# Transposing an 8192 x 8192 matrix: each DMA engine takes every sixteenth row of a chunk, and a permutation matrix on TensorE restores the order

## The chip, the cores and the metric

The kernel runs on one core of one Trainium2 chip. The metric is the device time in microseconds (us) of one execution; lower is better. The kernel before took 1264.38 us, the median of three runs between 1263.99 and 1264.57 us. Its profile comes from one execution of its own.

## The reference

```python
x = np.random.randn(8192, 8192).astype(np.float32)

def reference(x):
    return np.transpose(x)
```

Input and output are 268.4 MB each and both lie in HBM. There is no arithmetic to do: every number is read once, moved to its transposed place and written once.

## The kernel before

The matrix is cut into 128 chunks of 128 rows by 4096 columns (2 MB each): two column halves `s`, and 64 row blocks `c` in each. The list `chunks` (line 98) goes through all row blocks of the left half and then all of the right half. A chunk passes through four stages.

**Load** (`load`, lines 100 to 104). One DMA brings a chunk into one of three SBUF buffers `ins`, one row of x for each of the 128 partitions, 16 KB contiguous on both sides. The first three loads are issued on SP's queue, the other 125 on ScalarE's. Load t+3 is issued (lines 241 to 243) once TensorE has done the last transpose of chunk t, which frees the buffer.

**Transpose** (`transposes`, lines 111 to 124). TensorE waits for the chunk's load (line 112), then makes 32 transposes of 128 x 128: a matmul with the matrix `ident`, which GpSimd builds once at the start (lines 86 to 96). The chunk's columns are taken in 8 groups `q` of 512; within a group, transpose `b` takes every fourth column. The results go to PSUM, groups 0 to 3 to one half (`ps0`), 4 to 7 to the other (`ps1`); before each half TensorE waits until the half's last copies are done (line 116). TensorE runs this as a loop over three buffers (lines 138 to 149); the other engines' programs are written out in full.

**Copy** (lines 185 to 238). ScalarE copies the first half of PSUM, VectorE the second, into one of nine SBUF regions `regs`. A region gathers, for one group of 512 columns, what up to eight consecutive row blocks give, so that an output row gets a contiguous piece of up to 1024 numbers (4 KB). The group number sets at which row block its region closes (line 195), so that in the steady run about one region closes with each chunk. Before a region is filled anew, the copying engine waits until the region's last store has landed (line 202).

**Store** (`store`, lines 160 to 179). A closed region goes out as one DMA on ScalarE's queue. `wide_dma` (lines 25 to 36) writes the instruction directly, so that SBUF's side stays 16 KB contiguous per partition while the output's side has four rows of 4 KB. Only the first store is an ordinary one (line 174).

So loads and stores, but for the first three loads, are issued on ScalarE's queue, in the order of the program there: the copies of a chunk, the stores of the regions that these close, the next load. At the end SP waits for all stores (line 245).

The change touches the building of `ident` and `load`. What its steps meet are the DMA queues, the transposes of line 118 that read both, and the waits of lines 112, 202 and 242.

Of the kernel before, what the change touches and what calls it, by code (L numbers as in the profile page):

```python
# [40 lines left out]
def kernel(  # L41
# [14 lines left out]
    P = 128  # L56
# [8 lines left out]
    NIN = 3  # L65
    NREG = 9
    CH = N // P
    J = S * P

    with tc.tile_critical():  # L70
        nc.alloc_sbuf_tensor("pad", [P, 32], dt)
        ident = nc.alloc_sbuf_tensor("ident", [P, P], dt).ap()
        ins = [nc.alloc_sbuf_tensor(f"in{k}", [P, J], dt).ap() for k in range(NIN)]
        SIZE = B * W * P
# [10 lines left out]

        nc.gpsimd.memset(ident, 0.0).then_inc(s_id, 1)  # L86
        nc.gpsimd.wait_ge(s_id, 1)
        nc.gpsimd.affine_select(  # L88
            out=ident,
            in_=ident,  # L90
            compare_op=mybir.AluOpType.not_equal,
            fill=1.0,
            base=0,
            pattern=[[-1, P]],
            channel_multiplier=1,
        ).then_inc(s_id, 1)

        chunks = [(s, c) for s in range(M // J) for c in range(CH)]

        def load(t):  # L100
            s, c = chunks[t]
            (nc.sync if t < NIN else nc.scalar).dma_start(
                out=ins[t % NIN], in_=x[c * P:(c + 1) * P, s * J:(s + 1) * J]
            ).then_inc(s_ld[t % NIN], 16)


# [45 lines left out]
        for t in range(NIN):  # L152
            load(t)
# [6 lines left out]
        def store(q, e, count):  # L160
# [3 lines left out]
            for s, a, z in parts:  # L164
                rows = (z - a) * P
                j0 = s * J + q * B * P
                dst = out[j0:j0 + B * P, a * P:a * P + rows]
# [17 lines left out]
        for t, (s, c) in enumerate(chunks):  # L185
            for e in range(2):
# [3 lines left out]
                for q in range(e * NH, (e + 1) * NH):  # L190
# [13 lines left out]
                    k = [p[0] for p in parts].index(s)  # L204
                    base = r * SIZE + B * P * sum(z - a for _, a, z in parts[:k])
                    _, a, z = parts[k]
# [13 lines left out]
                for u in runs:  # L220
# [4 lines left out]
                    i = pss[e][:, u[0] * B * P:(u[-1] + 1) * B * P]  # L225
                    i = i.rearrange("p (l b i) -> p l b i", b=B, i=P)
# [14 lines left out]
            if t + NIN < T:  # L241
                nc.scalar.wait_ge(s_pe, (t + 1) * NR // 2)
                load(t + NIN)
# [32 lines left out]
```

## Time and profile before

| | before |
|---|---|
| median of three runs | 1264.38 us |
| the profiled execution: span from first to last instruction | 1261.2 us |
| TensorE matmul / weight load busy | 740.3 us (59%) / 719.8 us (57%) |
| VectorE / ScalarE busy | 302.7 us (24%) / 252.6 us (20%) |
| mean granted TensorE clock | 0.751 |
| DMA packets, bytes, mean rate | 39273, 536.97 MB, 426 GB/s |

The page comes from one execution; its span leaves out what lies before the first and after the last instruction. The kernel's time is some 3 us above that span. Busy time of an engine says how long it had work in hand, not that the kernel waited for it. DMA is not an engine with a program of its own: a transfer is issued by SP or ScalarE, waits in a queue, and is carried out by sixteen DMA engines together, each of them taking a share. The page shows how busy these sixteen were in 40 slices of the span, and how long a transfer took from its issue to its landing. Beside the page, the trace holds one record for each packet that a DMA engine moved, with its start, its length in time and its bytes, and one for each of the sixteen steps by which a transfer raises its semaphore. It does not say which of the sixteen a packet belongs to; since an engine's next packet starts 3 to 4 ns before the last one ends, the packets can be strung together into sixteen chains.

### The profile page before, as it was taken

The page shows a single profiled execution, that of the slowest core. Times are in us where ns is not written, and L with a number is a line of the kernel's source. Part 1 is how long each engine was busy: PE and PEld are TensorE (multiplying, and loading weights), DVE is VectorE, ACT ScalarE, POOL GpSimd, SP SyncE. Part 2 cuts the span into 40 slices and gives each one's busy share as a digit, 9 for nine tenths or more (in the row PEclk, how much of TensorE's full clock was granted, in tenths as well). Part 3 has the DMA queues.
Part 4 walks back from the last instruction along what each step waited for, and adds up shares of the span by engine and source line. Part 5 has one row for each costly group of instructions (what it writes and reads, how often), then busy time and mean ns, then how long its engine had stood idle before and what let it go on. Part 6 is the DMA issues. An engine that isn't in the chain of part 4 may idle for free. (4 is left out here: it accounts for less than half of the span.)

```text
span 1261.2 us, 9840 instructions
## 1 busy us (share of the span) xinstructions
PE 740.3 (59%) x4096; PEld 719.8 (57%) x4096; DVE 302.7 (24%) x250; ACT 252.6 (20%) x257; POOL 0.7 (0%) x6
## 2 busy tenths in 40 slices
PE   6555655665556565665555655656566655656561
PEld 6555555665556555655555655656566655656561
DVE  3322222222222222222222222222222222222220
ACT  3212121121111211122211121121111211122120
POOL 0000000000000000000000000000000000000000
PEclk9987867777776868687776777676867677777866
DMA  9999999999999999999999999999999999999998
GB/s 386 429 427 426 430 427 429 431 428 430 431 428 431 429 429 430 430 429 430 425 423 419 431 430 429 430 430 429 431 430 429 431 429 430 430 430 429 429 429 351
DMA packets 39273, 536.97 MB, mean 426 GB/s; under 512 B 4320, under 2 KB 4832, under 8 KB 6240
## 3 DMA queue, kind: packets, MB, share of 16 engines
q10 hardware_dynamic: 38832, 530.60, 98.9%
q1 hardware_dynamic: 432, 6.29, 1.2%
q14 instruction: 8, 0.07, 0.0%
q8 instruction: 1, 0.02, 0.0%
HBM read 268.44 MB, written 268.44 MB: 426 GB/s over the span
## 5 line engine op out<-in xcount | busy, mean ns | idle before, releaser
L118 PE MATMUL ps<-ident,in 128*128 128x128 f32 x4096 | 740.3, 363 | 492.9 <-PEq L116 492.9
L118 PEld LDWEIGHTS ps<-ident,in 128*128 128x128 f32 x4096 | 719.8, 220 | 513.2 <-issue 513.2
L228 DVE COPY regs<-ps 128x512 f32<-128x512 f32 (+3 forms) x250 | 302.7, 1246 | 932.4 <-PE ps L118 780.2
L228 ACT COPY regs<-ps 128x512 f32<-128x512 f32 (+3 forms) x256 | 251.3, 1015 | 980.9 <-PE ps L118 495.5
L228 ACT ACT_TABLE_LOAD x1 | 1.3, 1283 | 0.9 <-SPq L70 0.9
L88 POOL TENSOR_SCALAR_AFFINE_SELECT ident<-ident 128x128 f32<-128x128 f32 x1 | 0.3, 292 | 0.2 <-POOL ident L86 0.2
L86 POOL MEMSET ident<- 128x128 f32 x1 | 0.2, 204 | 0.5 <-SPq L70 0.5
L260 POOL MEMSET const-bfloat16-1.0<- 128x1 bf16 x1 | 0.1, 101 | 0.0
L260 POOL MEMSET const-uint8-127<- 128x1 uint8 x1 | 0.1, 101 | 0.0
L260 POOL MEMSET const-float32-0.0<- 128x1 f32 x1 | 0.1, 98 | 0.2 <-issue 0.2
L260 POOL MEMSET const-float32-1.0<- 128x1 f32 x1 | 0.1, 98 | 0.0
## 6 DMA issues: line engine op xcount, KB each, us to landing
in<-in_x_dram ACTq DMA_DIRECT2D x125, 2048.0 KB, 21.7
out_dram<-regs ACTq DMA_DIRECT2D x114, 2048.0 KB, 17.5
out_dram<-regs ACTq DMA_DIRECT2D x4, 1792.0 KB, 17.1
in<-in_x_dram SPq DMA_DIRECT2D x3, 2048.0 KB, 11.6
out_dram<-regs ACTq DMA_DIRECT2D x4, 1536.0 KB, 15.2
out_dram<-regs ACTq DMA_DIRECT2D x4, 1280.0 KB, 15.5
out_dram<-regs ACTq DMA_DIRECT2D x4, 1024.0 KB, 15.6
out_dram<-regs ACTq DMA_DIRECT2D x4, 768.0 KB, 16.5
```

Source lines behind the costliest of these rows:

```text
L86: nc.gpsimd.memset(ident, 0.0).then_inc(s_id, 1)
L88: nc.gpsimd.affine_select(out=ident, in_=ident, compare_op=mybir.AluOpType.not_equal, fill=1.0, base=0, pattern=[[-1, P]], channel_multipl ...
L118: tr = nc.tensor.transpose(pss[e][:, (g * B + b) * P:(g * B + b + 1) * P], ins[k][:, q * B * P + b:(q + 1) * B * P - B + b + 1:B], ident,)
L228: cp = nc.scalar.copy(out=o, in_=i) if e == 0 else nc.vector.tensor_copy(out=o, in_=i)
L260: nc = _bacc.Bacc("TRN2", target_bir_lowering=False, num_devices=1)
```

## The change

The source of a load is presented in another order. Before, partition p of a buffer receives row p of the chunk, and rows and partitions are both one dimension of 128. Afterwards the source has two dimensions for the rows, 16 outer ones in steps of one row and 8 inner ones in steps of sixteen rows; the destination stays 128 partitions in sequence. Partition 8k + i therefore receives row 16i + k. The diff's sense is that each of the sixteen DMA engines takes one k, that is every sixteenth row. The matrix with which TensorE transposes is no longer the identity but the permutation that puts the rows back: in row 8k + i its one stands in column 16i + k. So PSUM holds the same numbers as before, and everything behind it is the same. A helper `split` is added and not called.

```diff
+    E = 16
...
         nc.gpsimd.memset(ident, 0.0).then_inc(s_id, 1)
         nc.gpsimd.wait_ge(s_id, 1)
+        shaped = ident.rearrange("p (i k) -> p i k", k=E)
         nc.gpsimd.affine_select(
-            out=ident,
-            in_=ident,
+            out=shaped,
+            in_=shaped,
             compare_op=mybir.AluOpType.not_equal,
             fill=1.0,
             base=0,
-            pattern=[[-1, P]],
+            pattern=[[-1, P // E], [-(P // E), E]],
             channel_multiplier=1,
         ).then_inc(s_id, 1)

         chunks = [(s, c) for s in range(M // J) for c in range(CH)]
+
+        def split(a):
+            step, n = a.ap[0]
+            return bass.AP(a.tensor, a.offset, [[step * (n // E), E], [step, n // E]] + [list(d) for d in a.ap[1:]])

         def load(t):
             s, c = chunks[t]
             (nc.sync if t < NIN else nc.scalar).dma_start(
-                out=ins[t % NIN], in_=x[c * P:(c + 1) * P, s * J:(s + 1) * J]
+                out=ins[t % NIN],
+                in_=x[c * P:(c + 1) * P, s * J:(s + 1) * J].rearrange("(i k) j -> k i j", k=E),
             ).then_inc(s_ld[t % NIN], 16)
```

## The prediction

> **What bounds the kernel now.** I read the page's parts 2 and 3 first (slices and queues), then part 6 (issues), then the total of the waits, then windows cut around the stages.
>
> ```profile
> DMA  9999999999999999999999999999999999999998
> GB/s 386 429 427 426 430 427 429 431 428 430 431 428 431 429 429 430 430 429 430 425 423 419 431 430 429 430 430 429 431 430 429 431 429 430 430 430 429 429 429 351
> ...
> q10 hardware_dynamic: 38832, 530.60, 98.9%
> q1 hardware_dynamic: 432, 6.29, 1.2%
> ```
>
> The sixteen DMA engines are busy in every slice, and the two queues together take 100.1% of sixteen engines' span. The rate is flat near 430 GB/s, whatever the compute engines do. Nothing on TensorE, VectorE or ScalarE sets the end (59%, 24% and 20% busy on the page).
>
> ```profile
> in<-in_x_dram ACTq DMA_DIRECT2D x125, 2048.0 KB, 21.7
> out_dram<-regs ACTq DMA_DIRECT2D x114, 2048.0 KB, 17.5
> ...
> in<-in_x_dram SPq DMA_DIRECT2D x3, 2048.0 KB, 11.6
> ```
>
> A 2 MB load lands 21.7 us after its issue, though 2.097 MB at 430 GB/s is 4.9 us: it stands behind about 16.8 us of other transfers. The queue is over three transfers deep.
>
> ```profile
> ACT regs L228 <- PE ps L118: 495.5, 100, 9.2
> PE ps L118 <- PEq L116: 492.9, 127, 8.5
> ACT regs L228 <- DMA out_dram<-regs: 473.9, 60, 10.4
> ```
>
> In the totals of the waits, everything on the compute side waits for a transfer or for something that waited for one.
>
> ```profile
> 4.00:10.00 6.00, 1.00 1.01 434
> 300.00:400.00 100.00, 0.72 1.01 430
> 640.00:700.00 60.00, 0.72 1.01 421
> 1238.00:1248.00 10.00, 0.50 1.01 421
> ```
>
> These windows (start and end, us, granted clock, DMA share, GB/s) hold loads alone, the mix, the middle with its cut stores, and stores alone. Loads alone are no faster than the mix. So the end is the sum of the packets' times on one engine, and only a change in those can move it.
>
> The trace's single packet records give that sum. Each load puts 8 packets of 16,384 B on each engine; a packet takes 611 ns, and the next starts 3 to 4 ns before its end, so 0.607 us each. 128 loads are 1,024 packets, 622 us of an engine; the stores (2 at 611 ns, 6 at 616) are the same again. 622 + 627 = 1249 us; with first packets of up to 1.46 us, 9 ns for each semaphore write and 5.3 us by which the last engine lags at the end, this fills 1261.2 us. The median, 1264.38 us, is 3.2 us above this span; I carry those 3.2 us.
>
> **The change, part by part.**
>
> Identity (lines 86 to 96). The same single select of 128x128 on GpSimd with a two-dimensional pattern. Now 292 ns, over 1.66 us into the span; the first weight load waits for data until 8.43 us. Even if it doubled, 6.8 us of the first load cover it: 0.
>
> TensorE (lines 111 to 124). 4096 matmuls of 128x128 f32 before and after, same operands, same order, one matrix with its ones elsewhere: 0. They are 740.3 us in a span of 1261.2, behind loads.
>
> Issue of the loads. Three on SP's queue (1.32 us together) and 125 on ScalarE's (0.33 to 0.8 us each). The new source has three dimensions (16 by 8 rows by 4096), as the stores have at line 28, whose issue takes 0.55 us. Say +0.25 us each: 125 x 0.25 = 31 us on ScalarE's queue. Behind a load's issue stand the next ScalarE copies and store issues, which idle 473.9 + 495.5 us. The 16.8 us of queued transfers hide it; without that cover it would be the 31 us. The first load's issue alone is bare: +0.3 us.
>
> Packets of the loads, the one term that counts. A row's 4096 elements stay contiguous on both sides, so I expect 128 packets of 16 KB per load as now, 8 for each of 16 engines (16 divides the new outer 16 and the 128 partitions). [...]
>
> What the rows cannot say is which partitions an engine writes now. In the first load all sixteen engines start within 0.9 us and finish within 0.43 us of each other, and from the second packet on nearly all take 611 ns: marching in step, no two engines hinder each other. The source's rows and the 128 partitions are now cut alike, so any division of them is possible. Afterwards the outer source dimension is 16 against 128 partitions, and the only equal shares that respect both are one source index for each engine, hence a run of eight neighbouring partitions. If the present division is such runs too, nothing changes. If it is another, chosen so that no two engines meet at one entrance to SBUF, that is lost.
>
> Both ends of a packet's price: below, 611 ns stays (gain at most the 3 us mean of stretched packets, 421 records above 617 ns, 5.3 us on the last engine). Above, two engines share an entrance and each goes at half speed. From the records of 512 B (27 ns) and 16,384 B (611 ns), 15,872 B cost 584 ns: 603 ns for 16 KB plus 8 ns fixed. A shared packet is 2 x 603 + 8 = 1214 ns, so +603 ns x 1,024 = +617 us. [...] Landings of the first loads spread over 0.29 to 0.43 us, so the lead of the worst pair is between 0 and 0.43; I take 0.15: 2 x 0.15 x 128 = 38 us back. The slowest pair counts, since a load's semaphore needs all sixteen.
>
> I take the upper end, against the nearest row (611 ns), for two reasons in the rows. Packets of 16 KB cost 611 ns in loads and the first two of each store alike, and loads alone, the mix and stores alone run at 434, 430 and 421 GB/s. So the pace is set by something common to reading and writing SBUF that exists sixteen times, and the SBUF side fits as well as the engine itself. And freedom from collisions in step is what a deliberate division looks like.
>
> [...]
>
> Sum: 1261.2 + 3.2 + 0.3 + 617 - 38 = 1844 us, given as **1845 us**; with the lead between 0.43 and 0 us, 1772 to 1882.
>
> **The rivals.**
>
> No change, chance 0.30, 1264.4 us (1262 to 1267): the division keeps engines apart, because it is runs of eight already, or is taken from the SBUF side alone so that the change does not do what it says, or pairs drift apart for good. For it: every load packet is 611 ns now. Against it: the new shapes no longer match.
>
> Pairs meet but come apart, 0.13, 1267 to 1772: stretched packets already part the engines, and late loads land over 5.3 us. [...] Against it: a pair that runs free empties its queue within some three transfers, and starts the next beside the others again; through 300 us, eleven of sixteen engines land within 0.6 us.
>
> Reads disturbed in HBM, 0.07: sixteen engines read rows 32 KB apart instead of farther. If the whole span went at the 421 GB/s of the middle window instead of 430, 1249 x 430/421 is +27 us; for loads alone half, 1278.
>
> The other side, faster, 0.08, 1259 us: the stretched packets come from reads that meet in HBM, and the new rows end them. At most the 5.3 us by which the last engine lags go: 1264.4 - 5.3 = 1259.1. It decides only if load packets stay at 611 ns. Against it: stretching clusters at 60 to 128 and at 625 to 697 us, where stores are cut into uneven parts, and the load rows are no different there.
>
> **How the numbers follow.** Sharing in full 0.42 (1772 to 1882, the forecast's own range), in part 0.13, disturbed reads 0.07: slower 0.62. Same 0.30, faster 0.08; 0.2% is 2.5 us, about what a measurement of this kernel can tell from no change. The range runs from 1262 (all but the faster case) to 1882: 8 times in 10 cannot be had without both the no-change case and the full one.
>
> **What would show it.** Right: load packets near 1.2 us from the first load on, three SP loads that take about 29 us (24 packets of 1.21 us) instead of 15, a mixed rate near 290 GB/s with the DMA share still 9 in every slice, and store packets at 611 to 616 ns. ScalarE's issue of a load near 0.55 us. TensorE's matmul mean unchanged at about 363 ns but for the clock. No change: GB/s at 430 and load landings near 21.7 us. Wrong altogether if packets get smaller (more than 39,273 on the page), or fall on fewer than 16 engines, or if a compute engine is what a load waits for.

## The result and the profile after

The changed kernel is slower, by 4.2% in the comparison: ratio 1.042, 95% interval 1.039 to 1.046. Its six executions took 1312.8, 1317.4, 1323.4, 1765.3, 1820.8 and 1826.5 us, while six of the kernel before stayed between 1263.4 and 1264.6. The ratio counts only the shorter three; the profile shown here is of the execution of 1820.8 us (span 1819.0 us). The scatter belongs to the kernel: the same program, with the same data, ends in one of two ways, and both need an explanation.

The page of the changed kernel, parts 2 and 3:

```profile
DMA  9999999999999999999999999999999999999996
GB/s 217 278 327 327 344 308 321 335 302 304 290 288 294 297 299 297 288 294 292 294 287 291 291 284 288 295 290 297 288 287 288 291 300 293 291 289 287 299 295 279
...
q10 hardware_dynamic: 38832, 530.60, 97.6%
q1 hardware_dynamic: 432, 6.29, 1.6%
```

The DMA engines are as busy as before, the packets and bytes are the same (39273 packets, 536.97 MB), but the rate has fallen to about 290 GB/s. Nothing was added to move; what is moved takes longer. Part 6 and the totals of the waits follow from it:

```profile
in<-in_x_dram ACTq DMA_DIRECT2D x125, 2048.0 KB, 34.9
out_dram<-regs ACTq DMA_DIRECT2D x114, 2048.0 KB, 26.3
...
in<-in_x_dram SPq DMA_DIRECT2D x3, 2048.0 KB, 21.6
```

```profile
PE ps L125 <- PEq L123: 1029.2, 128, 13.8
ACT regs L235 <- PE ps L125: 803.0, 105, 13.6
ACT regs L235 <- DMA out_dram<-regs: 725.3, 59, 14.6
```

TensorE's wait for loads grew by 536 us (492.9 to 1029.2), nearly the whole loss of 558 us in the span. (The view names TensorE's own sequencer; in both traces the first transpose of a chunk starts 0.29 us, in the median, after the last landing of the chunk's load.) The windows (start and end, us, granted clock, DMA share, GB/s) with loads alone, twice the mix, and stores alone:

```profile
4.00:10.00 6.00, 1.00 0.98 208
300.00:400.00 100.00, 0.64 1.00 323
900.00:1000.00 100.00, 0.68 1.00 288
1795.00:1805.00 10.00, 0.50 1.01 424
```

Loads alone fell to half (434 to 208 GB/s); stores alone are unchanged (421 to 424). It is the loads, from the first one on. Their packet records say it most plainly: over the first three loads a packet takes 1212 ns in the mean (most between 1.07 and 1.29 us), against 639 ns in the mean and 611 ns in the median before. Stores keep 611 and 616 ns.

### The profile page after: what moved, and what is told of

It reads as the page before. It is cut to its first block, busy times and chain, and to the rows that moved or that the text cites. A ratio compares the mean times of both kernels' runs of the same rounds, so it can differ in the third digit from the quotient of the medians.

```text
span 1819.0 us, 9840 instructions
## 1 busy us (share of the span) xinstructions
PE 763.1 (42%) x4096; PEld 742.4 (41%) x4096; DVE 302.8 (17%) x250; ACT 252.9 (14%) x257; POOL 0.8 (0%) x6
## 2 busy tenths in 40 slices
DMA packets 39273, 536.97 MB, mean 295 GB/s; under 512 B 4320, under 2 KB 4832, under 8 KB 6240
## 5 line engine op out<-in xcount | busy, mean ns | idle before, releaser
L125 PE MATMUL ps<-ident,in 128*128 128x128 f32 x4096 | 763.1, 371 | 1029.2 <-PEq L123 1029.2
L125 PEld LDWEIGHTS ps<-ident,in 128*128 128x128 f32 x4096 | 742.4, 220 | 1049.6 <-issue 1049.6
```

The lines of the kernel that those rows point to most:

```text
L125: tr = nc.tensor.transpose(pss[e][:, (g * B + b) * P:(g * B + b + 1) * P], ins[k][:, q * B * P + b:(q + 1) * B * P - B + b + 1:B], ident,)
```

## The experiments

Theory A: with 16 by 8 rows the engines hinder each other in pairs while they load (1212 instead of 611 ns a packet), and a pair pays until one engine leads the other by enough. That an engine now writes eight neighbouring partitions, that the two meet at an entrance to SBUF, and that four packets (2.4 us at 0.607 us each) are enough, are assumptions of mine; no run shows them. Theory B: the rows' order in HBM disturbs the reads. Theory C: the way in which the instruction is written or issued costs the time. All executions, us, in order; those of the kernel before, taken beside them, lie between 1262.7 and 1269.2:

| label | what | times |
|---|---|---|
| e1 | changed kernel again | 1374, 1376, 1377, 1787, 1796, 1828 |
| e2 | only the shape of the source | 1313, 1328, 1335, 1586, 1638, 1777 |
| e3 | written out, 128 rows | 1262.5 to 1266.1 (ten) |
| e4 | every sixteenth row, 128 rows | 1263.4 to 1265.9 (ten) |
| e5 | small delay, groups of four | 1295, 1302, 1358, 1390, 1596, 1712 |
| e6 | small delay, groups of eight | 1333, 1342, 1383, 1410, 1421, 1817 |
| e7 | larger delay at the start | 1367, 1606, 1696, 1799, 1808, 1814 |
| e8 | delay at load 9, groups of four | 1402, 1404, 1788, 1795, 1814, 1823 |
| e9 | delay at load 9, groups of eight | 1370, 1394, 1415, 1775, 1792, 1821 |
| e10 | shape changed from load 24 on | 1310, 1314, 1314, 1344, 1350, 1680, 1714 |
| e11 | e10 with delay, groups of four | 1276, 1278, 1281, 1290, 1296, 1370, 1400, 1540 |
| e12 | e10 with delay, groups of eight | 1295, 1306, 1311, 1314, 1446, 1532, 1696 |

**e1, the changed kernel unaltered.**

> The changed kernel once more, unaltered. Theory A (two engines write through one entrance to SBUF while their eight neighbouring partitions are loaded, as long as one leads the other by less than four packets, 2.4 us): the first three loads take packets of 1.1 to 1.3 us as in the profile shown; from then on each execution depends on whether all pairs come apart, so single times scatter between about 1300 and 1830 us, and where the time is near 1315 us the rate climbs from 220 GB/s in the first 15 us to 430 GB/s within the first 200 us and the load packets return to 611 ns. Theory B (the rows' order in HBM disturbs the reads): loads stay slow evenly over the span, and times repeat within 1%.

The profiled execution had a span of 1374.2 us. Its page, part 2:

```profile
GB/s 208 258 285 333 290 301 312 315 331 337 358 402 422 430 432 428 430 432 428 429 432 424 409 417 426 430 431 429 428 431 429 430 431 428 429 433 427 429 426 353
```

A slice is 34 us. For eleven slices the rate is that of the long execution, then it climbs to 430 GB/s and stays, with a dip to 409 and 417 at the turn of the column halves. The loss is over by about 410 us, later than the 200 us expected; the shape is theory A's, and B's even slowness is excluded. Packet records tie the loss to the time: adding, over all 16 KB packets, what each took beyond 611 ns and dividing by sixteen engines gives 6.4 us before, 117.6 us here and 544.9 us in the profile after, so 111 and 539 us more than before. The spans are longer by 113 and 558 us.

**e2, the shape alone.**

```diff
+            if t < NIN:
+                ld = nc.sync.dma_start(out=ins[t % NIN], in_=rows)
+            else:
+                rows = rows.rearrange("(k i) j -> k i j", k=16)
+                ld = wide_dma(nc, nc.scalar, "qActDynamicHW", ins[t % NIN], rows)
```

> The kernel before with its rows in their old order and the plain identity; only the source of the 125 loads on ScalarE's queue is written as 16 by 8 rows instead of 128. The first three loads stay as before. Theory A: as the changed kernel, 1300 to 1830 us, scattered, packets of loads at 1.1 to 1.3 us from the fourth load on. Theory B: 1264 us, since each row goes to the same partition as before and the rows read are the same.

Measured: 1313 to 1777 us, scattered like the changed kernel, though each partition receives the row it received before. Windows of the profiled execution (span 1326.0 us):

```profile
2.00:14.00 12.00, 1.00 1.00 408
20.00:60.00 40.00, 0.78 1.01 249
60.00:100.00 40.00, 0.71 1.00 299
100.00:150.00 50.00, 0.65 1.01 331
150.00:200.00 50.00, 0.76 1.00 328
200.00:300.00 100.00, 0.73 1.01 417
300.00:400.00 100.00, 0.78 1.01 429
```

In the first 14 us the three old loads still run at 408 GB/s; with the new shape the rate is 249, and it returns by 300 us. Theory B fails: no row changed its place. In the same window, 20 to 60 us, e1 had 238 GB/s: its copies have the same shape with the rows in another order.

**e3, the same way of writing with 128 rows.** As e2, without the line that regroups the rows.

> The kernel before, with the same 125 loads written out in the same way as in e2 but with 128 rows in one dimension. Theory A: 1264 us within 0.2%, load packets 611 ns, though ScalarE's issue of a load rises to the stores' 0.55 us. Theory C (the way the instruction is written or issued costs the time): as e2.

Ratio 0.9998 (0.9989 to 1.0007). Theory C fails. The shortest issues of a load on ScalarE's queue rise from 0.33 us to 0.50 us, and cost nothing.

**e4, every sixteenth row with 128 rows in one dimension.**

```diff
+            rows = x[c // 16 * 2048:(c // 16 + 1) * 2048, s * J:(s + 1) * J]
...
+                out=ins[t % NIN], in_=rows.rearrange("(p k) j -> k p j", k=16)[c % 16]
```

> The kernel before, loading into partition p the row 16p + k of a block of 2048 rows, so that each engine reads every sixteenth row while rows and partitions are both one dimension of 128. The output's columns stand in another order than the reference's. Theory A: 1264 us, at most 1270, load packets 611 ns. Theory B: slower by about as much as the changed kernel, 1315 us or more.

Ratio 1.0007 (0.9998 to 1.0016). Reading rows sixteen apart costs nothing, and brings nothing either. Part 2 of the pages of e3 and e4, one line of each:

```profile
GB/s 384 428 426 427 430 429 430 428 430 429 429 431 429 429 429 429 430 430 429 428 425 416 430 428 430 430 430 429 429 429 430 430 430 430 429 429 429 431 409 331
```

```profile
GB/s 379 421 423 427 428 430 430 429 429 429 430 429 430 430 428 430 431 430 430 428 425 417 430 430 429 432 430 428 431 429 430 430 431 429 429 431 428 429 430 361
```

Both are flat near 430 but for the ends and the turn of the column halves, as before. What is left is how a copy of 16 by 8 rows is shared out among the engines. The next experiments ask who shares with whom.

**e5 and e6, delays ahead of the first load.** The changed kernel, with small copies within HBM issued on SP's queue, of 4, 8 and 12 pieces of 80 KB. I took a copy of n pieces to occupy n engines, and the smaller copies to take engines that the larger ones take too. Numbered by that, engines 0 to 3 start three pieces late, 4 to 7 two, 8 to 11 one, 12 to 15 at once; the trace does not say which engine is which, so the numbers are only names for these groups. A piece is five packets, 3.0 us at 0.607 us each, an estimate. The pairs e and e+4 are an assumption, put to the test here:

```diff
+        for n in (4, 8, 12):
+            part = x[16 * base:16 * (base + n), :J].rearrange("(a z) j -> a z j", z=16)
+            nc.sync.dma_start(
+                out=spare[base:base + n, :5, :], in_=part[:, :5, :]
+            ).then_inc(s_sp, 16)
+            base += n
```

For e6 the list is `(8,)`: one copy of 8 pieces, so that engines 0 to 7 would start one piece behind 8 to 15.

> [...] Theory A with the pairs e and e+4: every pair is parted by more than four packets from the first load on and stays so; load packets at 611 ns, three loads without the 1.1 to 1.3 us packets, all times between 1268 and 1290 us and within 1% of each other. If what parts pairs is not their lead, or the pairs are others: as the changed kernel, 1300 to 1830 us, scattered.

> [...] Theory A with the pairs e and e+4: no pair is parted, since both of each pair are late by the same; packets of 1.1 to 1.3 us in the first loads, times scattered between 1300 and 1830 us. With the pairs e and e+8, or if any late start of some engines helps: as e5, 1266 to 1280 us, without scatter.

The delays reach groups of the sizes that were meant: packets under 512 B, the semaphore writes among them, are 24 more in e5 than in the kernel before (4344 against 4320), as many as the copies have pieces. In e5 the sixteen landings of the first load stand in four groups of four, the first of each 1.9, 2.3 and 1.6 us behind the first of the one before; in e6 in two of eight, 1.6 us apart, and still so at the third load. But my times for e5 were wrong (1295 to 1712 us, not 1268 to 1290); those for e6 were right. In e5, with groups 1.6 to 2.3 us apart, packets were still stretched in part. Windows of e5 and e6 over the second and third load show the difference:

```profile
15.00:28.00 13.00, 1.00 1.01 305
```

```profile
15.00:28.00 13.00, 0.98 1.01 217
```

In e6 nearly all packets of these two loads take 1.15 to 1.29 us: a lead of 1.6 us between the engines that the copy of eight delays and the other eight parts nobody. In e5 four packets of one engine in the third load take 799, 1156, 876 and 611 ns: 3.44 us where 2.44 is the free price (4 x 0.611) and 4.85 the shared one (4 x 1.212).

**e7, a larger delay in the same place.** Pieces of eight packets instead of five: by 0.607 us each, 1.8 us more between the groups than the 1.6 to 2.3 us of e5, so some 3.4 to 4 us, an estimate.

```diff
-                out=spare[base:base + n, :5, :], in_=part[:, :5, :]
+                out=spare[base:base + n, :8, :], in_=part[:, :8, :]
```

> As e5 with pieces of 128 KB instead of 80 KB. [...] Theory A: among the first three loads, which follow each other without stores, a lead of 3.4 to 4.0 us is as good as one of 0.9 to 1.5 us (a load is 4.9 us long), so they still share in part; once loads and stores alternate every pair is free, the rate reaches 425 GB/s within 100 us, and all times lie between 1270 and 1295 us, within 1% of each other but for single executions in which a pair falls together again at the turn of the column halves. If a lead does not end the sharing: as the changed kernel, 1300 to 1830 us, scattered.

This failed: 1367 to 1814 us. It was no test. The first load's landings are spread over 12.9 us as intended, the fourth load's over 0.8 us: between the first loads and the first stores the queues run empty (at 34 us some 5 of the sixteen engines are at work), the engines wait, and begin again together.

**e8 and e9, delays behind load 9.** The copies of e7, 128 KB a piece, now on ScalarE's queue; e9 has `(8, 8)`.

```diff
                 load(t + NIN)
+            if t == 6:
+                part((4, 12))
```

> In e7 the leads did not last: the fourth load landed on all sixteen engines within 0.8 us, since after the first three loads the queues ran empty and the engines began again together. So the changed kernel now gets its small transfers later, on ScalarE's queue behind load 9, where transfers stand in line: of 4 and of 12 pieces of 128 KB. Engines 0 to 3 fall back by 16 packets, 4 to 11 by 8, 12 to 15 by none, so both e and e+4 of every pair get 8 packets, 4.9 us, between them. Theory A with the pairs e and e+4: pairs still within 2.4 us of each other are parted to 2.4 to 7.3 us, which is free; the rate goes to over 400 GB/s within some 100 us of it, five of six times or more lie between 1285 and 1360 us. If a lead does not end the sharing: as the changed kernel, half or more of the times above 1360 us.

> The same place and the same longest delay, but twice 8 pieces: engines 0 to 7 fall back by 16 packets, 8 to 15 by none. Theory A with the pairs e and e+4: no pair is parted; times scatter as the changed kernel's, 1300 to 1830 us, half or more of them above 1360 us. If the pairs are e and e+8, or if any disturbance parts pairs: as e8.

e8 failed too (1402 to 1823), and does not differ from e9, so that e9's times, though as expected, tell nothing either. Its landings tell why it could not work: before the delay came, the sixteen landings of loads 3 to 9 were already spread over 0.5, 0.7, 1.1, 1.9, 3.4, 6.3 and 9.6 us, at load 9 eight engines still within 0.4 us of each other, eight ahead of them by 0.5 to 9.6 us. A delay of 4.9 us on top can bring a pair together as well as part it.

**e10 to e12, the new shape from load 24 on.** e10 is e2 with `t < 24` in place of `t < NIN`, so that loads and stores alternate and most engines are in step when the shape changes (at load 23 of e10, fourteen of the sixteen landings lie within 0.8 us, the last two 2.3 and 3.4 us behind the first). e11 adds the copies of e8 right ahead of load 24, and e12 those of e9:

```diff
+                if t + NIN == 24:
+                    part((4, 12))
                 load(t + NIN)
```

> In e8 the pairs were already 1 to 9 us apart, some engines ahead and some behind, when the delay came, so it could bring pairs together as well as part them. Here the first 24 loads are those of the kernel before, and only from load 24 on, about 250 us into the span, is the source written as 16 by 8 rows (rows in their old order, plain identity). Until then all engines march in step in a steady alternation of 8 load and 8 store packets. Theory A: 430 GB/s up to load 24, under 330 GB/s right behind it, then each execution for itself: times scatter between 1280 and 1735 us (104 loads of at most 4.5 us more).

> As e10, with transfers of 4 and 12 pieces of 128 KB right ahead of load 24: e and e+4 of every pair are 4.9 us apart, half a cycle of 16 packets, when the new loads begin. Theory A with pairs e and e+4: no sharing at all, load packets stay at 611 ns, over 420 GB/s behind load 24, all six times between 1270 and 1295 us (the delay itself is up to 9.8 us). If the lead does not end the sharing, or falling together is what pairs tend to: as e10.

> As e11, with twice 8 pieces: the same longest delay, but both engines of each pair e and e+4 are late by the same. Theory A with those pairs: under 330 GB/s right behind load 24 and times as scattered as e10's. With pairs e and e+8: their lead is 9.8 us, a whole cycle, so the same as e10; with no pairs but any disturbance helping: as e11.

Windows of e10, e11 and e12 before, at and behind load 24:

```profile
150.00:200.00 50.00, 0.73 1.01 428
215.00:235.00 20.00, 0.66 1.00 288
235.00:260.00 25.00, 0.64 1.02 322
```

```profile
150.00:200.00 50.00, 0.73 1.01 429
215.00:235.00 20.00, 0.66 1.01 410
235.00:260.00 25.00, 0.77 1.00 421
```

```profile
150.00:200.00 50.00, 0.78 1.01 429
215.00:235.00 20.00, 0.59 1.00 315
235.00:260.00 25.00, 0.77 1.02 308
```

The three programs are alike up to load 24. At load 24 the landings of e11 stand in groups of four, eight and four, some 5 us from one to the next, with three single engines that lag by 3 us, as three did before the delay; those of e12 stand in two groups of eight, some 10 us apart, each within 2.4 us. Without a delay the rate falls to 288, with a delay by eights to 315, with one by fours it stays above 410. Of the 16 KB packets between 222 and 262 us, 966 of 1034 take at most 620 ns in e11, but 385 of 764 in e10 and 327 of 744 in e12, where the unstretched ones are mostly the stores. e12 alone does not exclude pairs across the two halves, since 10 us between them is about a whole cycle of 16 packets, as good as no lead; e6 does, where the halves stood 1.6 us apart and the loads still took 9.7 us each. Together they settle the pairs: each has one engine in a lower and one in an upper group of four, in the same half of the sixteen, and about 5 us between them end nearly all the sharing. The runs do not show which of the four upper engines is whose partner, so that e and e+4 remain an assumption, nor that the place where two engines meet is at SBUF.

The times agree only in part. The ratios of the shorter times are 1.0383 (95% interval 1.0365 to 1.0401) for e10, 1.0103 (1.0085 to 1.0120) for e11 and 1.0367 (1.0346 to 1.0388) for e12. Five of e11's eight times lie between 1276 and 1296 us, about where all were expected, and three do not: pairs part and fall together again later. In its profiled execution (span 1294.2 us) stretched packets return at 275 to 350 us and, at the turn of the column halves, from 650 to 875 us.

## Why the prediction was wrong

- **The bound, the covers and the issues** were right. DMA stays at 9 in every slice but the last, matmuls take 371 ns in the mean, the permutation costs nothing (GpSimd's select took 340 instead of 292 ns, and nothing waits for it), and the longer issue of the loads (0.61 us) is hidden; e3 shows that by itself. Two readings were off without weight: single issues of a load took up to 4.6 us before, not 0.8, and the stores' sum by its own figures is 625 us, not 627.
- **The packet's price** was right, and it was the choice against the nearest row: 1214 ns forecast, 1212 ns measured over the first three loads. So was, as far as the runs go, the mechanism behind it: loads of 128 rows in one dimension keep about 430 GB/s (e3, e4), loads of 16 by 8 rows fall to 249 (e2, 20 to 60 us), and it is pairs of engines that pay (e5, e6, e11, e12). That the pairs meet at an entrance to SBUF was assumed; no run shows it.
- **The failed step is the lead.** I took 0.15 us for the slowest pair from the first loads of the kernel before and held it for all 128 loads. That a load gets cheaper by twice the lead, which gave the term of -38 us and the 1772 of the range, no run shows; e5 showed in its place four packets at 3.44 us, between 2.44 free and 4.85 shared, with groups 1.6 to 2.3 us apart. Against parting I argued that "a pair that runs free empties its queue within some three transfers, and starts the next beside the others again". Leads do not keep still. Even in the kernel before, where load packets keep 611 ns, the landings spread over 0.3 us at load 6 and over 3.4 us at load 16, which I could have read. In the changed kernel the spread grows by half or more with each load (0.5 to 9.6 us over loads 3 to 9 of e8); e5 shows the sharing in part where groups stood 1.6 to 2.3 us apart, e11 next to none at about 5 us, and in e1 and e2 it ends for good but for the turn. That makes the term +53 us in the executions that the ratio counts (1317 against 1264; +112 in the shorter ones of e1), where I had +579. It is the rival "pairs meet but come apart", to which I gave 0.13 and 1267 to 1772 us.
- **Where the forecast does describe an execution**, it is the long kind. In the profile after, from 376 us on, the last two landings of every load come 16 to 24 us behind the first and mostly 0.2 us behind one another, to the end: by their landings, two engines in step. The other fourteen share as well: between 400 and 1700 us 12,446 packets take over 700 ns, more than the some 11,600 that the loads have in that time, and on average only about 0.1 of sixteen engines has nothing in hand. That the last two set the pace, and the others reach the end of the queue and start the next transfer together, as the sentence quoted says, fits this but is not shown. Eight packets of 1212 instead of 611 ns are 4.81 us more for a load, 615 us for 128; the span is 558 us longer. That the last two stand about as close as my 0.15 us is luck, since the other leads moved. Of the six long executions of after and e1, 1765 to 1828 us, five lie in the 1772 to 1882 that I gave for full sharing. What I did not see is that both ends are possible for one program.
- **Faster and unchanged** were rightly the lesser cases: e4, with rows sixteen apart, wins nothing.

Open is what makes a lead grow. If the two shared evenly, it would stay as it is. Open too is why a last pair does not part as the others do, and what brings pairs together again in e11. An attempt to hold all leads in place over the whole span was not made.

No version here beats the kernel before; e11, at best 1276 us where e10 without the delay has 1310, only shows how much of the loss can be avoided by keeping pairs apart.

## What to carry to other kernels

When transfers bound a kernel, the outermost dimension of a copy's source can decide how it is shared out among the engines, even where every row keeps its partition (249 GB/s in e2 at 20 to 60 us, about 430 in e3); before regrouping rows, check that packets still take their free time when all engines march in step, as in the first loads of a run (1212 against 639 ns in the mean here). If the order of the rows must change, change it in a way that leaves the 128 partitions against 128 rows, as e4 does (about 430 GB/s, ratio 1.0007). And when one program's times scatter while its neighbour's do not, look for engines that can be in or out of step, and take several profiles before putting a price on it.

## What the runs showed of the hardware beyond that

- A busy share of 100% says nothing about the pace: it stood at 0.98 to 1.01 with 208, 290 and 430 GB/s, since a stretched packet counts as busy for 1.21 us (mean of the first three loads after) instead of 0.61.
- Sharing is graded: in e5, where groups stood 1.6 to 2.3 us apart, four packets of one engine take 0.80, 1.16, 0.88 and 0.61 us, between the free price of 0.61 and the shared one of 1.21.
- Small copies with n outer pieces delayed groups of n engines (four groups of four in e5, landings 1.6 to 2.3 us apart; two of eight in e6, 1.6 us apart): a means to set the phase of DMA engines against each other.
- Rows sixteen apart, 512 KB from one partition's row to the next, read at the same 430 GB/s as neighbouring rows (e4).
